# Down as seven whole products, its right parts made in gate/up, and layer 1's later modulation moved

## The chip, the cores and the metric

The kernel runs on one core of a Trainium2 chip. The metric is the device time of one execution in microseconds (us). Three executions of the kernel before took 2651.18 us in the median (2650.96 to 2657.16). One more execution was recorded by the profiler; it took 2657.73 us, of which the profile shows a span of 2656.0 us, at a granted TensorE clock of 0.974. All views of the trace come from that one. Engines: PE is TensorE's matmul, PEld its weight load, DVE VectorE, ACT ScalarE, POOL GpSimd, SP SyncE (here it issues nearly all DMAs, in the order in which they stand in its queue).

## The reference

Two layers of an encoder, one sequence of 1024 rows, width 1024, FFN width 2816, all in fp32:

```python
cond = silu(c)
for l in range(2):
    mod = cond @ w_mod[l] + b_mod[l]
    sh_a, sc_a, gt_a, sh_f, sc_f, gt_f = split(mod, 6)      # six groups of 1024
    h = rms_norm(x, g_attn[l]) * (1 + sc_a) + sh_a
    qa, ka, va, qb, kb, vb, qc, kc, vc = split(h @ w_in[l])
    ya = neighborhood_attention(qa, ka, va, rpb_na[l])       # group A
    yb = sliding_window_attention(qb, kb, vb, sink_sw[l], t5_table)   # group B
    yc = axial_attention(qc, kc, vc, gq_ax[l], gk_ax[l])     # group C
    y = concat(rms_norm(ya), rms_norm(yb), rms_norm(yc))
    x = x + gt_a * (y @ w_o[l])
    h = rms_norm(x, g_ffn[l]) * (1 + sc_f) + sh_f
    gate, up = split(h @ w_gu[l], 2)
    x = x + gt_f * ((silu(gate) * up) @ w_down[l])           # "down"
return rms_norm(x, g_final)
```

The six groups of `mod` are numbered (layer, 0) to (layer, 5) below: (1,0) and (1,1) are the shift and scale of layer 1's attention norm, (1,2) is the gate of its output projection, (1,3) to (1,5) belong to its FFN.

## The kernel before

**Numbers.** TensorE multiplies fp32 data in a faster form of lower precision (`F32R`), so each operand is split into a high part (a copy in `F32R`, made by ACT) and a low part (the source minus the high part, made by DVE or POOL): `split_to`, line 195. One product of tiles is three matmuls, high·high, low·high and high·low (`mm3`, line 187). The activations are kept transposed: rows of a tile are features (128 of them, a "block"), columns are the 1024 sequence positions in two halves of 512.

**Strassen–Winograd.** Gate/up and most of down don't compute the four quadrant products (feature blocks in pairs, sequence in halves) as eight multiplications but as seven, with sums of quadrants on both sides: `PRODUCTS`, line 203, gives for each of the seven its number, the name of its right part (`11`, `21`, `22`, `t1` to `t4`; the t are sums and differences of the quadrants b11, b12, b21, b22 of the right operand) and the PSUM bank into which it is added (a, b or c). `a_parts`, line 211, makes the seven left parts from raw weight tiles. `Ahead`, line 239, keeps up to eight such parts made ahead of the product that uses them; they live in the eight buffers of the tag `whl` (tiles `wpt`). Raw weights pass through the two buffers of `wst` (tiles `wr`, `wst`).

**Order.** Each engine runs its instructions in order. The order is what a scheduler makes of the program, except between `pin(..., True)` and `pin(..., False)`, where the order of the code is kept on the named engines. PSUM has eight banks, shared under the tag `mm` by all of `ps_w`, `ps_d`, `ps_mod`, `ps_ab` and so on.

**A layer's stages, in order.** Normed input h; projections of C (`ps_c`) and V (`ps_v`), then A and B (`ps_ab`, `ab_proj`/`ab_split`, whose results `qko` go to DRAM by `store()`); attention; output projection; gate/up; down; and the norm for the next stage.

**Modulation.** A group of `mod` takes eight steps (`mod_step`, line 283): a load of 128x1024 of `w_mod` (tile `wmt`, 512 KB; or two of 128x512) and a DVE operation that multiplies it by a scalar column of cond and adds it to `acc`. Then `acc` is split (`mod_parts`), summed over partitions on PE by a matmul with ones (`ps_mod`), picked on DVE by multiplying with the identity and reducing, and the bias is added (`mod_flush`, `mod_finish`). `mod_next` does a step each time it is called, the load and its use together. It is called in layer 0's V and A/B projections, its output projection and its gate/up, and there the six groups of layer 1 are made too.

**Gate/up.** 22 column groups q (even: gate, odd: up), each of 7 products of 12 matmuls. A pair of q gives 256 features of `silu(gate)*up`: the quadrants b11, b12 in a tile `e`, b21, b22 in a tile `o` (both `sg` in the trace), which `g_store` writes to DRAM (`gd`, 512 KB each).

**Down before.** 18 of the 22 feature blocks go through the seven products: for each of three stretches `kb` of 6 blocks, `g_load` reads them back (three loads of 1 MB, `graw`), `g_part` makes the seven right parts (sums and splits, on DVE and POOL in turn), and for `np2` in 0, 1 the weights of four output blocks are loaded in pieces of 384 KB and summed (`a_parts`, `dn_sums`). After every product its bank is added to the residual stream at once (`residual`, DVE `xb<-ps_w,mod,xb`, times the gate of the FFN): 84 of these a layer. The last 4 blocks are multiplied plainly (`down`, `down_block`; `ps_d`, 192 matmuls and 32 residuals). Half 0 of the next norm, or of the final norm, is started beside the last of these.

The part of the gate/up loop and of down that sets what runs when:

```python
for i, p in enumerate(PRODUCTS[2 if q < EARLY else 0 :]):
    gu_product(q, p, ahead.get())
    ahead.fill()
    if q + 1 < NF:
        g_store()
    elif i == 0:
        pin([sp], True)
    if i % 2 == 0 and l == 0 and q > 1:
        mod_next(psl, (ntp, "sq", 2, H))
```

## Time and profile before

| what | value |
|---|---|
| median of three runs | 2651.18 us |
| profiled execution / its span | 2657.73 / 2656.0 us |
| gate/up of layer 0 / layer 1, from its first product part to the last matmul | 471 us (631.80 to 1103.07) / 452 us (1925.00 to 2377.39) |
| down of layer 0 / layer 1 | 262 us (1103.07 to 1364.83) / 265 us (2377.39 to 2642.10) |
| C and V projections of layer 1 | 132 us (1364.83 to 1496.70) |
| A/B projections of layer 0 / layer 1 | 72 us (191.9 to 264.3) / 68 us (1496.70 to 1564.60) |
| after layer 1's down | 14 us |

How to read the rows that follow: a row of the engine totals gives busy time, share of the span and the number of instructions. In the groups, `out<-in` names the tiles without buffer numbers, `L47` is the line of the recording helper through which every operation passes (so all have the same line, and groups are told apart by their tiles), and behind the bars stand busy time and mean ns of one, then the engine's idle time ahead of them and what ended most of it. The chain of waits is followed back from the last instruction. The windows view gives start and end in us from the span's start. Sizes of the transfers that matter here:

```profile
gd<-sg SPq DMA_DIRECT2D x44, 512.0 KB, 3.1
graw<-gd SPq DMA_DIRECT2D x18, 1024.0 KB, 5.7
wmt<-in_w_mod_dram SPq DMA_DIRECT2D x98, 256.0 KB, 2.9
```

### The profile page before, as it was taken

Reading aid. Unit: us, or ns where it says so; the run is one execution under the profiler, and the core shown is the slowest. Engines: PE = TensorE matmul, PEld = TensorE weight load, DVE = VectorE, ACT = ScalarE, POOL = GpSimd, SP = SyncE. Lnnn points to the kernel's source line nnn. Section 1 sums busy time; section 2 is a strip of 40 time slices with the busy share of each in tenths; the row PEclk is TensorE's granted clock in tenths of the full one; section 3 lists DMA queues with packets and bytes.
Section 4 is the critical chain, followed back from the end, with each engine's and each line's share of the span. In section 5 each row is a group of like instructions: output and inputs, shape, how many; then the busy total and the mean of one; then the engine's idle time right before and its main releaser. Section 6 shows DMA issues by size and latency. Waiting matters only on the chain.

```text
span 2656.0 us, 34702 instructions
## 1 busy us (share of the span) xinstructions
PE 2481.2 (93%) x12055; PEld 2028.6 (76%) x12055; DVE 1918.7 (72%) x2964; ACT 1236.8 (47%) x2345; POOL 1193.6 (45%) x1039
## 2 busy tenths in 40 slices
PE   6899999898899999989999999999989999998898
PEld 4677898777688787667777879987867888876677
DVE  6845999987877777598778149998684443449876
ACT  5421888833433333343233148886444333334332
POOL 5641445543644444464345224455454444446431
PEclk9999999999999999999999999999989999998999
DMA  8467215074344554522233531241623222252222
GB/s 260 147 187 223 67 25 154 21 236 149 105 149 151 164 166 135 188 98 92 92 104 86 128 115 25 62 122 60 215 63 111 79 96 64 91 185 89 95 80 79
DMA packets 233566, 316.10 MB, mean 119 GB/s; under 512 B 29752, under 2 KB 166160, under 8 KB 233392
## 3 DMA queue, kind: packets, MB, share of 16 engines
q1 hardware_dynamic: 233088, 313.75, 37.9%
q8 instruction: 95, 1.56, 0.2%
q14 instruction: 79, 0.65, 0.1%
q0 software_dynamic: 304, 0.14, 0.0%
HBM read 244.24 MB, written 70.55 MB: 119 GB/s over the span
## 4 chain that ended last, share of the span: by engine, by line
PE 63%; DVE 23%; issue 4%; DMA 4%; ACT 3%; POOL 2%; SPq 0%; POOLq 0%; DVEq 0%; ACTq 0%
PE ps_w L47 29%; PE pv L47 6%; PE ps_ab L47 5%; PE ps_o L47 5%; PE T L47 4%; DVE xb L47 4%; PE ps_v L47 3%; PE sC L47 3%; PE ps_d L47 3%; DVE ws L47 2%; DVE wpt L47 2%; DMA wmt<-in_w_mod_dram 2%; DVE graw L47 2%; DVE acc L47 1%; PE sA L47 1%
## 5 line engine op out<-in xcount | busy, mean ns | idle before, releaser
L47 POOL TENSOR_SCALAR pr<-pr,rs 128x1024 f32<-128x1024 f32 (+4 forms) x256 | 208.8, 818 | 223.6 <-DVE rs L47 207.8
L47 POOL TENSOR_TENSOR wlo<-wst,whi 128x1024 fp32r<-128x1024 f32 x66 | 164.6, 2497 | 299.9 <-ACT whi L47 261.8
L47 POOL TENSOR_TENSOR wpt<-ws,wpt 128x512 fp32r<-128x512 f32 (+1 forms) x136 | 179.9, 1326 | 259.6 <-ACT wpt L47 215.4
L47 ACT CAST wpt<-ws 128x512 fp32r<-128x512 f32 (+1 forms) x272 | 155.8, 583 | 164.0 <-PE ps_w L47 77.5
L47 PE MATMUL pv<-pt,vs 128*128 128x256 f32 x1216 | 201.7, 297 | 11.3 <-DVE y L47 4.9
L47 POOL TENSOR_TENSOR wpt<-wr,wpt 128x512 fp32r<-128x512 f32 (+1 forms) x92 | 130.5, 1420 | 175.9 <-ACT wpt L47 150.5
L47 DVE TENSOR_TENSOR pt<-T,pt 128x512 fp32r<-128x512 f32 x304 | 199.4, 680 | 10.3 <-ACT pt L47 8.8
L47 PE MATMUL T<-identr,pr 128*128 128x128 f32 x1320 | 192.6, 275 | 4.9 <-POOL pr L47 1.9
L47 DVE TENSOR_TENSOR ws<-wr 128x512 f32<-128x512 f32 (+1 forms) x136 | 125.0, 925 | 92.0 <-POOL wpt L47 78.0
L47 ACT CAST pt<-T 128x512 fp32r<-128x512 f32 x304 | 170.1, 587 | 41.7 <-PE T L47 39.8
L47 POOL TENSOR_TENSOR sg<-sg,u 128x512 f32<-128x512 f32 x88 | 127.1, 1444 | 137.1 <-ACT u L47 68.1
L47 PEld LDWEIGHTS pv<-pt,vs 128*128 128x128 f32 x1216 | 161.5, 190 | 25.8 <-DVE y L47 12.7
L47 PEld LDWEIGHTS T<-identr,pr 128*128 128x128 f32 x1320 | 157.2, 141 | 27.1 <-POOL pr L47 4.4
L47 ACT COPY u<-ps_w 128x512 f32<-128x512 f32 x132 | 77.4, 586 | 215.7 <-PE ps_w L47 215.7
L47 DVE SCALAR_TENSOR_TENSOR acc<-wmt,condT,acc 128x512 f32<-128x512 f32 (+1 forms) x113 | 129.3, 1152 | 56.3 <-DMA wmt<-in_w_mod_dram 55.7
L47 DVE TENSOR_TENSOR wpt<-ws,wpt 128x512 fp32r<-128x512 f32 (+1 forms) x136 | 116.9, 860 | 64.4 <-ACT wpt L47 64.3
L47 DVE SCALAR_TENSOR_TENSOR xb<-ps_w,mod,xb 128x512 f32<-128x512 f32 x168 | 123.5, 742 | 48.3 <-PE ps_w L47 48.2
L47 ACT CAST wpt<-wr 128x512 fp32r<-128x512 f32 (+1 forms) x184 | 105.3, 578 | 112.1 <-PE ps_w L47 97.8
L47 ACT CAST whi<-wst 128x1024 fp32r<-128x1024 f32 x82 | 85.6, 1049 | 129.3 <-PE ps_o L47 40.5
L47 PE MATMUL ps_w<-ht3h,wpt 128*128 128x512 f32 x352 | 113.8, 405 | 17.4 <-ACT sg L47 16.0
L47 DVE TENSOR_REDUCE rs<-sC 128x1 f32<-128x1024 f32 x96 | 116.9, 1220 | 10.1 <-PE sC L47 9.8
L47 PE MATMUL ps_w<-ht2h,wpt 128*128 128x512 f32 x352 | 114.2, 405 | 7.7 <-ACT wpt L47 3.1
(332 smaller groups left out, 7127.2 us busy)
## 6 DMA issues: line engine op xcount, KB each, us to landing
wr<-in_w_gu_dram SPq DMA_DIRECT2D x92, 512.0 KB, 3.6
wmt<-in_w_mod_dram SPq DMA_DIRECT2D x98, 256.0 KB, 2.9
qk<-qkd SPq DMA_DIRECT2D x44, 512.0 KB, 7.2
gd<-sg SPq DMA_DIRECT2D x44, 512.0 KB, 3.1
wr<-in_w_down_dram SPq DMA_DIRECT2D x48, 384.0 KB, 3.6
graw<-gd SPq DMA_DIRECT2D x18, 1024.0 KB, 5.7
qkd<-qko SPq DMA_DIRECT2D x64, 256.0 KB, 3.5
wst<-in_w_o_dram SPq DMA_DIRECT2D x32, 512.0 KB, 4.2
```

Of the source, the lines that this page charges most:

```text
L47: ins = op(*args, **kwargs)
```

## The change

Four things change. In numbers for the whole program: matmuls in down go from 948 to 924 a layer, DVE's instructions from 2966 to 2898, POOL's from 1044 to 886, and SP's DMAs from 800 to 992.

**Down's loops.** The seven products run one after the other, in a new order (`DOWN`: numbers 1, 2, 6, 7, 4, 5, 3), each over all 22 feature blocks (11 pairs t) and four output blocks j. A step is a "unit", 77 in all: one left part and one right part of 128x512 are split (ACT and DVE; POOL isn't used), and 12 matmuls go into four banks. Products 1, 6, 7 and 4 share four banks (`acc_a`), 2, 5 and 3 the other four. A product's banks are added to the residual stream when it ends: 28 residuals a layer instead of 116.

**Weights.** All quadrants of the weights are loaded once, as 256 KB tiles `W[name, t]` that stay in SBUF (44 tiles, and 11 of `22` read a second time by `w_again`); the four sums are made in place on DVE (`w_sums`, `w_sum4`), at units that the table `due` names.

**Right parts.** The sums and differences of b11 to b22 are made in gate/up (`g_steps`, four subtractions on DVE per pair of column groups), and seven parts of 256 KB are stored to `gpd` in place of two of 512 KB to `gd`. Down reads them two units at a time (`b_load`, 512 KB) into the two buffers of `wst`.

**Modulation.** In gate/up `mod_stream` takes the place of `mod_next`: it issues each load one step ahead of its use, and stops ahead of group (1,2). The groups (1,2) to (1,5) are made in layer 1 instead, in the loops of its V and A/B projections, with three calls of `mod_next` after each A/B projection (layer 0 has one call there, as before). The norm of half 0 (`early_half`) runs beside products 5 and 3, and so do the squares of odd blocks of half 1.

The core of the diff:

```diff
+    DOWN = (
+        (1, "11", "a"), (2, "21", "b"), (6, "t2", "a"), (7, "t3", "a"), (4, "t4", "a"),
+        (5, "t1", "c"), (3, "22", "c"),
+    )
+    PLACE = {p[1]: i * NB for i, p in enumerate(DOWN)}
...
+    def mod_stream(psp, shared, until):
+        pl, tag, bufs, width = shared
+        acc = None
+        while todo and todo[0] < until:
+            l, g = todo[0]
...
+            if halves:
+                load(0)
+                yield
+            for i, (k, c0) in enumerate(halves):
+                if i + 1 < len(halves):
+                    load(i + 1)
+                mod_add(k, acc[:, c0 : c0 + width], loads.pop(i))
+                yield
+            going["step"] = KC
+            mod_parts(slice(0, width), shared)
+            yield
+            while going["step"]:
+                mod_flush(psp)
+                yield
...
-            if l == 0 and t > 1:
-                mod_next(psl, (ab, "zt", 4, 1024))
+            if t > 1:
+                mod_next(psl, (ab, "zt", 4, 1024), l)
...
-                for _ in range(1 - l):
-                    mod_next(psl, (ab, "zt", 4, 1024))
+                for _ in range(1 + 2 * l):
+                    mod_next(psl, (ab, "zt", 4, 1024), l)
...
+        def g_steps(b, e, o):
+            b11, b12, b21, b22 = (t[:, i * H : (i + 1) * H] for t in (e, o) for i in range(2))
+            def put(name, src):
+                sp.dma_start(gpd[:, PLACE[name] + b, :], src)
+            due = {
+                0: lambda: [put(*a) for a in (("11", b11), ("22", b22), ("21", b21))],
+                6: lambda: sub(b11, b12, b11),
+                7: lambda: (sub(b12, b22, b12), sub(b22, b22, b11), put("t1", b11)),
+                8: lambda: (sub(b21, b21, b22), put("t3", b12), put("t2", b22)),
+                9: lambda: put("t4", b21),
+            }
...
             for i, p in enumerate(PRODUCTS[2 if q < EARLY else 0 :]):
                 gu_product(q, p, ahead.get())
                 ahead.fill()
-                if q + 1 < NF:
-                    g_store()
-                elif i == 0:
-                    pin([sp], True)
-                if i % 2 == 0 and l == 0 and q > 1:
-                    mod_next(psl, (ntp, "sq", 2, H))
+                g_step()
+                if i % 2 == 0 and q > 1:
+                    next(mods_due, None)
...
+        def b_load(i):
+            n = min(2, NU - 2 * i)
+            t = wp.tile([P, 2, H], F32, name="graw", tag="wst", bufs=2)
+            sp.dma_start(t[:, :n], gpd[:, 2 * i : 2 * i + n, :])
+            for k in range(n):
+                raw[2 * i + k] = t[:, k]
+        A_SRC = ("11", "12", "11", "21", "11", "22", "12")
+        def units():
+            for u in range(NU):
+                i, t = divmod(u, NB)
+                both = []
+                for src in (W[A_SRC[i], t], raw.pop(u)):
+                    d = wp.tile([P, 2, H], F32R, name="wpt", tag="whl", bufs=8)
+                    split_to((d[:, 0], d[:, 1]), src, dve)
+                    both.append(d)
+                yield both
+        def w_sums(t):
+            w11, w21, w22 = (W[name, t] for name in ("11", "21", "22"))
+            dve.tensor_tensor(out=w22, in0=w21, in1=w22, op=ALU.add)
+            sub(w21, w11, w21)
+            sub(w11, w22, w11)
...
+        for t in range(NB):
+            at_unit(t, lambda t=t: w_first("12", t, wbp))
+            at_unit(4 + 2 * t, lambda t=t: w_first("21", t, wap))
+            at_unit(4 + 2 * t, lambda t=t: w_first("22", t, wbp))
+            at_unit(8 + 2 * t, lambda t=t: w_sums(t))
+            at_unit(31 + t, lambda t=t: w_sum4(t))
+            at_unit(33 + t, lambda t=t: w_again(t))
...
+        pin([sp], True)
+        for t in range(NB):
+            w_first("11", t, wap)
+            if t in (1, 3):
+                b_load(t // 2)
+        ahead = Ahead(units())
+        ahead.fill(4)
+        g_step(len(steps))
+        xt = blocks(xp)
+        b_load(2)
...
+        for u in range(NU):
+            i, t = divmod(u, NB)
+            num, _, bank = DOWN[i]
+            for what in due.get(u, ()):
+                what()
+            ahead.fill(4)
+            if u % 2 == 0 and (u + 6) // 2 <= (NU - 1) // 2:
+                b_load((u + 6) // 2)
...
+            banks = acc_a if bank == "a" else acc_b
+            a, b = ahead.have.pop(0)
+            for j in range(4):
+                js = slice(j * P, (j + 1) * P)
+                mm3(
+                    banks[j], a[:, 0, js], a[:, 1, js], b[:, 0], b[:, 1],
+                    num in (1, 2, 5) and t == 0, t == NB - 1, skip_group_check=True,
+                )
+            next(beside, None)
...
+            for j in range(4):
+                residual(banks[j], 2 * j + m, slice(half * H, half * H + H), 40)
+            if num == 4:
...
+                beside = chain(early_half(), odd_squares())
```

**Where down starts, on SP.** The first place at which the order differs is the end of layer 1's gate/up and the start of its down, in SP's queue of DMAs. Before (`wr` are raw weights, `graw` loads of the FFN's activations, `xb` blocks of the residual stream):

```order
L47 DMA wr<-in_w_gu_dram 128x4x256
L47 DMA xb<-xd 128x1024
L47 DMA graw<-gd 128x2x1024 x3
L47 DMA wr<-in_w_down_dram 128x3x256 x2
L47 DMA gd<-sg 128x1024 x2
L47 DMA xb<-xd 128x1024 x4
```

After the change (with buffer numbers; `sg_20511` is the last `e`, `sg_20512` the last `o`, `w11` the left weights of product 1):

```order
L49 DMA gpd_94<-sg_20511 128x512
L49 DMA gpd_94<-sg_20512 128x512
L49 DMA w11_20767<-in_w_down_dram 128x4x128
L49 DMA w11_20769<-in_w_down_dram 128x4x128
L49 DMA gpd_94<-sg_20512 128x512
L49 DMA graw_20771<-gpd_94 128x1024
L49 DMA w11_20773<-in_w_down_dram 128x4x128
L49 DMA w11_20775<-in_w_down_dram 128x4x128
L49 DMA graw_20777<-gpd_94 128x1024
```

The loads of the first activations stood ahead of the last two stores and read earlier blocks; now the third store of the last pair (part `21`) stands ahead of the first load of right parts.

**The same place, on DVE.** After the change, DVE's rows around that store (`u` are the results of an up product, `ps_w` its bank; the multiplication that finishes part `21` is the row `sg_20512<-sg_20512,ps_w_20645`):

```order
L49 TENSOR_TENSOR u_20691<-u_20691,ps_w_20693 128x512
L49 TENSOR_TENSOR sg_20511<-sg_20511 128x512
L49 TENSOR_TENSOR sg_20511<-sg_20512,sg_20511 128x512
L49 TENSOR_TENSOR sg_20512<-sg_20512,sg_20511 128x512
L49 TENSOR_TENSOR sg_20512<-sg_20512,ps_w_20645 128x512
L49 TENSOR_TENSOR wpt_20793<-w11_20767,wpt_20793 128x512
L49 TENSOR_TENSOR sg_20512<-sg_20512 128x512
L49 TENSOR_TENSOR wpt_20796<-graw_20771,wpt_20796 128x512
```

Three subtractions that overwrite b11, b12 and b22 stand ahead of the multiplication of the last product; the first split of a weight part stands between it and the fourth subtraction.

**Layer 1's A/B stage, on DVE.** The second place is behind the last split of V in layer 1 (`vs`). Before:

```order
L47 CAST qk<-pk 128x128
L47 TENSOR_TENSOR vs<-ps_v,vs 128x8x64 x8
L47 SCALAR_TENSOR_TENSOR qko<-ps_ab,qko 128x512 x12
L47 TENSOR_REDUCE rs<-sC 128x1 x2
L47 RECIPROCAL rs<-rs 128x1 x2
```

After the change the steps of a modulation group (`acc<-wmt,condT`) and its end stand between the results of the A/B projections (`qko`), and three more groups like it follow:

```order
L49 TENSOR_TENSOR vs<-ps_v,vs 128x8x64 x8
L49 TENSOR_SCALAR acc<-wmt,condT 128x1024
L49 SCALAR_TENSOR_TENSOR acc<-wmt,condT,acc 128x1024 x2
L49 SCALAR_TENSOR_TENSOR qko<-ps_ab,qko 128x512
L49 SCALAR_TENSOR_TENSOR acc<-wmt,condT,acc 128x1024 x5
L49 CAST acch<-acc 128x1024
L49 TENSOR_TENSOR accl<-acc,acch 128x1024
L49 TENSOR_TENSOR acc<-ps_mod,identr 128x512 x2
L49 TENSOR_REDUCE sums<-acc 128x4 x2
L49 TENSOR_TENSOR mod_83<-sums,vecs_81 128x8
```

On PE each of these groups puts four `ps_mod` matmuls between the A/B matmuls; the first stands behind 24 of them, the further ones 72, 72 and 48 apart.

342 lines of the change are left out of this document (147 added, 195 removed).

## The prediction

> **What bounds the kernel now.** I read the page first: its engine totals and its chain of waits.
>
> ```profile
> span 2656.0 us, 34702 instructions
> PE 2481.2 (93%) x12055; PEld 2028.6 (76%) x12055; DVE 1918.7 (72%) x2964; ACT 1236.8 (47%) x2345; POOL 1193.6 (45%) x1039
> PE 63%; DVE 23%; issue 4%; DMA 4%; ACT 3%; POOL 2%; SPq 0%; POOLq 0%; DVEq 0%; ACTq 0%
> ```
>
> PE carries 63% of the chain and DVE 23%, so the question for each stage is where the 23% sits. The windows view, cut at the first and last matmul of each stage, answers that: start and end, length, then the busy time of PE, PEld, DVE, ACT and POOL, the granted clock, DMA share and GB/s.
>
> ```profile
> 631.80:761.30 129.50, 108.21 (x437) 85.34 (x436) 107.66 (x120) 54.49 (x92) 67.59 (x42) 0.92 0.35 112
> 761.30:1085.80 324.50, 321.73 (x1379) 258.74 (x1378) 243.55 (x304) 119.05 (x211) 142.67 (x97) 1.00 0.48 154
> 1925.00:2045.50 120.50, 106.85 (x433) 84.74 (x432) 87.06 (x97) 52.35 (x90) 64.06 (x41) 0.93 0.27 89
> 2045.50:2360.20 314.70, 314.70 (x1356) 255.10 (x1356) 130.06 (x157) 120.21 (x211) 130.43 (x97) 1.00 0.26 85
> 1103.07:1364.83 261.76, 234.08 (x962) 182.11 (x960) 221.74 (x294) 96.23 (x177) 119.10 (x84) 0.96 0.31 103
> 2377.39:2642.10 264.71, 240.99 (x991) 187.91 (x990) 225.16 (x297) 94.30 (x176) 112.97 (x81) 0.95 0.27 93
> 1364.83:1496.70 131.87, 126.32 (x577) 101.61 (x576) 83.72 (x113) 45.39 (x87) 65.74 (x56) 0.96 0.38 102
> 1496.70:1564.60 67.90, 67.90 (x293) 54.65 (x292) 8.94 (x14) 12.05 (x18) 10.54 (x5) 1.00 0.49 131
> ```
>
> Rows 1 and 2 are gate/up of layer 0, rows 3 and 4 the same of layer 1, rows 5 and 6 down of the two layers, row 7 the C and V projections of layer 1, row 8 its A/B projections. Gate/up of layer 1 is a pure PE stage from 2045 on. Down is not: PE idles 28 and 24 us there and DVE is busy 85% of it. The A/B row has PE at 100% and DVE almost free.
>
> **The change part by part.**
>
> *Down, PE.* From the chain of waits, in order of time, two long unbroken stretches give the price of a matmul (start, length, count):
>
> ```profile
> 2009.18 362.80 PE ps_w L47 x1560
> 2594.11 34.00 PE ps_d L47 x150
> ```
>
> 362.8/1560 is 0.2326 us; 34.0/150 is 0.2267. Before, a layer's down has 756 matmuls in products and 192 plain ones, 948; after, 77 units of 12, 924. At 0.2326 a unit is 2.79 us and 77 of them 214.9 us (209.5 at the lower price). So the matmuls saved are worth only 6 us; the rest of the 262 and 265 us is waiting, and what matters is whether DVE keeps up.
>
> *Down, DVE.* It gains 2 splits a unit (154), 44 weight sums and 28 residuals: 226 instructions a layer; it loses 116 residuals, the sums and differences of the right parts, and its share (half each, POOL has the rest) of the splits of right and weight parts. POOL loses all its work in down. The tile view gives min/median/max of such a 128x512 operation in ns:
>
> ```profile
> L47 DVE TENSOR_TENSOR graw<-graw x36: 674/683/1787, 1111.9 to 2523.5; 128x512 f32<-128x512 f32 x36
> L47 DVE TENSOR_TENSOR ws<-wr 128x512 f32<-128x512 f32 (+1 forms) x136 | 125.0, 925 | 92.0 <-POOL wpt L47 78.0 <-DMA wr<-in_w_gu_dram 9.3 <-DMA wr<-in_w_down_dram 1.8
> L47 DVE SCALAR_TENSOR_TENSOR xb<-ps_w,mod,xb 128x512 f32<-128x512 f32 x168 | 123.5, 742 | 48.3 <-PE ps_w L47 48.2
> ```
>
> The median is 0.683, the mean of another group 0.925, and the largest 1.79. Residuals, one of whose sources is PSUM, never vary (0.742). I take 0.69, because POOL will be idle: 198 x 0.69 + 28 x 0.742 is 157 us of 215. The busy part is products 1 to 3: there DVE has 72 splits, 44 sums and 12 residuals, 128 operations, 89 us against 33 units or 92 us, with four units made ahead as a cushion. So it fits, barely. At 0.925 it would not: 118 us, a rival below.
>
> The Trainium skill, SBUF — State Buffer, "Who interferes with whom", says that a DVE operation with two SBUF inputs and a GpSimd operation that reads SBUF lock each other out for a whole instruction. By it the spread is POOL's doing and down would run at the low price, as summed; without it 0.925 would be as good a choice, and the sum 36 us longer. The spread in the trace fits it; no row here shows a down without POOL.
>
> *The start of down is a new wait.* On SP the third store of the last up block's tiles stands ahead of the first load of the right parts. It waits for the last product of gate/up, whose DVE multiplication now stands behind three subtractions; one of them waits until the store of block 22 has landed. From the timeline and the DMA table:
>
> ```profile
> 1102.84 0.39 PE L47 MATMUL ps_w<-ht4l,wpt 128*128 128x512 f32 x1
> 1101.33 1.54 POOL L47 TENSOR_TENSOR sg<-sg,u 128x512 f32<-128x512 f32 x1 [0.28 <-DVE u L47]
> t<-gd SPq DMA_DIRECT2D x16, 256.0 KB, 3.0
> wr<-in_w_gu_dram SPq DMA_DIRECT2D x92, 512.0 KB, 3.6
> L47 ACT CAST wpt<-ws x272: 506/620/630, 674.4 to 2573.3; 128x512 fp32r<-128x512 f32 x88, 128x384 fp32r<-128x384 f32 x48
> ```
>
> The last matmul ends at 1103.2; the store of 22 can go at about 1101.1 and lands 3.0 later; two operations of 0.69 bring DVE to 1105.5; issue of the store and of the load take until 1106.3; 3.6 to land, 0.62 for ACT's cast: unit 0 starts at about 1110.6, 7.4 us late, and units 2 and up follow from the next load. What PE does after such a gap is in the trace too:
>
> ```profile
> 1977.23 1.22 PE L47 MATMUL ps_w<-ht3h,wpt 128*128 128x512 f32 x2 [6.55 <-ACT sg L47]
> 1977.23 4.90 PE ps_w L47 x12
> ```
>
> After 6.55 us of idling 12 matmuls took 4.90 us, 2.1 more than 12 x 0.2326. Start: 7.4 + 2.1, near 10 us in each layer (bounds 0, if the load overtakes, and 14).
>
> *Other waits in down.* Product 7 adds into the banks that product 6 has just filled, 4 after 7 and 3 after 5: each first matmul waits for a residual. Four residuals take 3.0 us, the other three banks' matmuls 2.1: 1 us each, 3. Transfers: in the first 28 units about 24 MB (44 weight blocks, 18 loads of two units, 8 of x), 24/88 us or 270 GB/s. The trace moved more:
>
> ```profile
> 1097.00:1101.00 4.00, 4.00 (x19) 3.22 (x18) 0.43 (x1) 1.73 (x3) 2.54 (x2) 1.00 1.02 417
> ```
>
> so I take it as hidden but for 2 us a layer (bounds 0 and 10). The norm beside products 5 and 3 costs PE 8 small matmuls in layer 0, about 2 us with its wait, and 32 transposes in layer 1, 4 us.
>
> Layer 0: 215 + 10 + 3 + 2 + 2 = 232, against 261.8: **-30**. Layer 1: 215 + 10 + 3 + 2 + 4 = 234, against 264.7: **-31**. The tail behind it keeps its chain of residual, square, sum, scale and store: 0.
>
> ```profile
> 2642.10:2656.00 13.90, 4.73 (x41) 4.20 (x39) 5.67 (x10) 2.93 (x6) 3.71 (x3) 0.79 0.41 151
> ```
>
> *Between the layers.* Half 0 is now normed inside down; before, PE waited for its last chunks and for the second sum:
>
> ```profile
> 1374.45 1.62 DVE ssq L47
> 1379.55 4.37 PE ps_c L47 x12
> ```
>
> 12 matmuls in 4.37 us show PE slow after that wait, which is behind the chunks of half 0 and eight sums on DVE. In the change four squares are made by ACT and summed by PE, behind 24 matmuls that cover them: **-5** (bounds 0 and -9).
>
> *Gate/up.* Layer 0 sheds four of its six modulation groups. Its steady part was 324.5 against 314.7 in layer 1; two groups remain, with each load issued a step ahead of its use: **-8**. The early part differs by 9 more, but that comes from steps ahead of it, which stay:
>
> ```profile
> 629.52 2.69 DVE acc L47
> ```
>  Both layers gain 4 subtractions per 14 products (2.7 us in 39); DVE is 41% busy in layer 1, so PE hides them; +1 for the early rows, where it is not.
>
> *The moved modulation.* Layer 1's A/B stage now gets 32 loads of 512 KB and four groups of DVE work. Layer 0's A/B stage has the same work thinner (min/median/max of that stage alone, then one group's end; the rows at 1496.74 and on `ps_ab` say what layer 1 has):
>
> ```profile
> L47 DVE SCALAR_TENSOR_TENSOR acc<-wmt,condT,acc x15: 1274/1276/3306, 194.1 to 263.6; 128x1024 f32<-128x1024 f32 x15
> DMA to landing us min/median/max: 3.9/5.4/7.5
> 252.87 0.69 DVE L47 CAST acch<-acc 128x1024 fp32r<-128x1024 f32 x1
> 253.67 1.22 DVE L47 TENSOR_TENSOR accl<-acc,acch 128x1024 fp32r<-128x1024 f32 x1
> 256.54 1.29 DVE L47 TENSOR_TENSOR acc<-ps_mod,identr 128x512 f32<-128x512 f32 x2 [1.64 <-PE ps_mod L47]
> 257.75 1.27 DVE L47 TENSOR_REDUCE sums<-acc 128x4 f32<-128x512 f32 x2
> 177.38 19.65 SPq L47 DMA_DIRECT2D wmt<-in_w_mod_dram  x7
> 1496.74 0.69 DVE L47 TENSOR_TENSOR vs<-ps_v,vs 128x512 fp32r<-128x512 f32 x1 [4.91 <-ACT vs L47]
> L47 PE MATMUL ps_ab<-hl,whi x256: 387/393/628, 93.8 to 1562.9; 128*128 128x512 f32 x128
> ```
>
> PE's order puts each group's four ps_mod matmuls behind 24, 72, 72 and 48 A/B matmuls, and PE goes in order: it waits there for the group's last step. DVE starts when the last V block is split, 0.7 us into row 8 (1497.4). Its chain to the fourth ps_mod: 28 steps at 1.28 and 4 first ones at 0.75 (38.8), four ends of 0.69 + 1.22 + 1.29 + 1.27 with 1.2 of waiting for PE (22.7, less 4 of the last one, which come behind its matmuls), 9 low halves of projections at 0.69 (6.2), and some 7 us where POOL's weight splits stretch a step to 3.3 as above: 71 us, to 1568. Then 72 matmuls (16.7) and 2 us of slow PE: 1587, where row 8's PE ends at 1562.9. **+25.** Loads keep up: four buffers, 5.4 to land and 1.3 to use, one every 1.7 us against the chain's 2.2. Bounds: +4, the 16 ps_mod matmuls alone, if DVE hid the rest; +45 at one load every 3 us.
>
> Sum: -30 - 31 - 5 - 8 + 1 + 25 = **-48 us** on the span of 2656.0, so 2608. The profiled execution took 2657.7 (span and 1.7 around it), 6.5 more than the median of the runs, 2651.2; on that median, **2603 us**.
>
> **The rivals.**
>
> *DVE binds down.* If sums and splits cost 0.925 though POOL is idle, products 1 to 3 take 118 us instead of 92, less a cushion of 8: 18 us a layer, 2639. For it: DVE has 3% to spare there. Against: medians of 0.68 beside a busy POOL. 0.14.
>
> *The moved modulation is hidden.* DVE had 59 of 68 us free in that stage; if PE's waits shrink to the 16 matmuls, 2582. Against: the first ps_mod comes after one projection block, 5.6 us, and needs eight steps. 0.08.
>
> *The start of down is not late.* If the loads overtake the stores, 20 us less: 2583. Against: SP's order. 0.08.
>
> *Slower.* The modulation loads of the A/B stage go one at a time: on SP each three stand between stores of qko halves that wait for DVE, so buffers that are free are filled late. One at a time a load costs 5.4 + 0.4 + 1.3, 7.1 us; 28 of them are 199, and the stage ends 130 us later than I have it: 2733. It decides from about 4.4 us a load, where the time passes 2659. For it: SP is in order. Against: layer 0 issued seven in 20 us on the same queue. 0.06.
>
> **How the numbers follow.** My own case (2590 to 2625) has 0.64, the rivals 0.14, 0.08, 0.08 and 0.06. The range of 2578 to 2642 takes in the two faster rivals, the lower matmul price and the DVE rival. A measurement here tells 0.3%, 8 us. Faster by more: all but the slower rival and part of DVE's case, 0.88; within: 0.06; slower: 0.06.
>
> **What would show it.** In down of the changed kernel: units 2.79 us apart, PE idle about 7 us ahead of the first, the wait ending in ACT's cast or the load of graw; DVE's 128x512 operations at 0.69 with POOL empty; residuals 28 a layer. In layer 1's A/B stage: PE idle ahead of each ps_mod on DVE, the first about 10 us, the stage near 92 us long. Wrong it would be if down is longer than 245 us, or if the A/B stage stays under 75.

## The result and the profile after

The changed kernel took 2649.16 us in the median of 20 runs (2637.84 to 2656.60) and the kernel before 2652.38 us in the same series: a ratio of 0.9985, interval 0.9974 to 0.9997. That is 3 us faster, just clear of the noise, where 48 were forecast. The profiled execution took 2648.72 us. The page of the changed kernel, with the span, the engine totals (busy time, share, instructions) and the shares of the chain of waits, answers to the first lines of the prediction:

```profile
span 2646.6 us, 34697 instructions
...
PE 2467.0 (93%) x12071; PEld 2037.8 (77%) x12071; DVE 1809.6 (68%) x2896; ACT 1241.2 (47%) x2335; POOL 964.5 (36%) x881
...
PE 50%; DVE 6%; issue 4%; DMA 2%; ACT 2%; POOL 1%; SPq 1%; POOLq 0%; DVEq 0%; ACTq 0%
```

The totals say that DVE and POOL have less to do and that PE is busy just as large a part of the time. They don't say why the time stayed. (The chain isn't comparable as a whole: its shares add up to 66% here, and near the end it runs through stretches in which POOL had nothing to do.) The windows view of the changed kernel, cut at each stage's last matmul, does. Rows: full products of layer 0's gate/up, layer 0's down, layer 1's C and V projections, its A/B projections, the full products of its gate/up, its down, the tail.

```profile
761.50:1110.60 349.10, 337.96 (x1437) 272.15 (x1435) 190.36 (x242) 120.79 (x214) 138.96 (x100) 0.99 0.35 113
1110.60:1334.80 224.20, 213.96 (x938) 175.81 (x938) 162.23 (x253) 102.87 (x178) 12.88 (x10) 0.98 0.66 198
1334.80:1479.40 144.60, 134.96 (x606) 109.93 (x605) 71.62 (x101) 42.91 (x83) 61.50 (x52) 0.92 0.40 112
1479.40:1584.00 104.60, 81.95 (x306) 62.94 (x305) 72.45 (x73) 11.02 (x16) 13.43 (x5) 0.85 0.70 226
2070.70:2402.60 331.90, 331.90 (x1429) 268.89 (x1427) 152.72 (x192) 121.08 (x214) 134.37 (x100) 1.00 0.29 96
2402.60:2628.00 225.40, 217.63 (x968) 179.22 (x967) 157.10 (x246) 98.98 (x173) 4.27 (x3) 0.98 0.64 190
2628.00:2646.60 18.60, 9.92 (x73) 9.34 (x71) 4.38 (x8) 3.54 (x7) 3.71 (x3) 0.66 0.30 113
```

Layer 0's gate/up before, cut in the same way (the prediction's row ends sooner, at 1085.80):

```profile
761.30:1103.00 341.70, 338.93 (x1453) 272.60 (x1452) 245.39 (x307) 123.16 (x218) 148.23 (x102) 1.00 0.50 160
```

Set against the profile before, from each stage's last matmul to the next one's:

| stage | before | after | difference | forecast |
|---|---|---|---|---|
| up to the end of layer 0's output projection | 631.9 | 630.9 | -1.0 | 0 |
| gate/up 0, first products / full products | 129.4 / 341.7 | 130.6 / 349.1 | +8.6 | -8 |
| down 0 | 262.0 | 224.3 | -37.7 | -30 |
| C and V of layer 1 | 131.1 | 144.5 | +13.4 | -5 |
| A/B of layer 1 | 67.2 | 104.6 | +37.4 | +25 |
| attention and output projection 1 | 361.9 | 362.5 | +0.6 | 0 |
| gate/up 1, first products / full products | 120.3 / 331.8 | 124.2 / 331.9 | +4.0 | +1 |
| down 1 | 264.8 | 225.4 | -39.4 | -31 |
| tail | 13.9 | 18.6 | +4.7 | 0 |
| sum | 2656.0 | 2646.6 | -9.4 | -48 |

The gain in down came, and was larger than forecast: 77 us. Five other rows gave 68 us of it back, 37 of them the A/B stage. (On the medians the change is worth 3 us instead of the 9.4 of these two executions; executions of one kernel differ by that much.)

**The A/B stage** is where most of it went. The timeline of PE in the changed kernel (start, length, operation; in brackets idle time before it and what ended it) at the ps_mod matmuls of the first three groups:

```profile
1494.01 1.22 PE L49 MATMUL ps_mod<-acch,onesr 128*128 128x512 f32 x2 [8.99 <-DVE acch L49]
...
1519.15 1.19 PE L49 MATMUL ps_mod<-acch,onesr 128*128 128x512 f32 x2 [5.44 <-DVE acch L49]
...
1542.21 1.22 PE L49 MATMUL ps_mod<-acch,onesr 128*128 128x512 f32 x2 [2.42 <-DVE acch L49]
```

PE waits for DVE's groups, as forecast, 22.5 us in all. But DVE waits too. The groups of DVE in that stage, with idle time ahead of them in the last column:

```profile
L49 DVE SCALAR_TENSOR_TENSOR qko<-ps_ab,qko 128x512 fp32r<-128x512 f32 x11 | 7.6, 690 | 22.6 <-ACT qko L49 22.6
...
L49 DVE TENSOR_TENSOR acc<-ps_mod,identr 128x512 f32<-128x512 f32 x8 | 5.2, 686 | 2.9 <-PE ps_mod L49 2.9
```

DVE stood idle 22.6 us ahead of the low halves of projections, some 12 of them before its fourth group was done. All but 1.5 of these 12 fall behind the first ps_mod: there DVE waited for projections that PE was late with, since PE had waited for DVE's group before it began them.

**The C stage** has a new wait. The chain of waits in it (start, length, what):

```profile
1366.49 1.30 POOL hl L49
1367.81 0.37 SPq L49
...
1368.82 12.00 DMA cst<-const_rope_dram
```

The last chunk of the norm ends on POOL at 1367.8, and only then SP issues the loads of the q/k gains and rotary constants, which take 12.00 us to land. That is 33 us behind the end of down (1334.8). Before the change the same loads went out 9 to 15 us behind it (1364.8), ahead of the norm's chunks of half 1:

```profile
1376.14 3.38 SPq L47 DMA_DIRECT2D cst<-const_rope_dram  x5
```

**Layer 0's gate/up** has stalls that layer 1's, with the same products and stores, doesn't have. The longest, in the timelines of DVE, ACT and PE:

```profile
916.18 2.49 DVE L49 TENSOR_TENSOR sg<-sg 128x512 f32<-128x512 f32 x2 [1.18 <-POOL sg L49]
918.59 0.68 DVE L49 TENSOR_TENSOR sg<-sg,ps_w 128x512 f32<-128x512 f32 x1
919.19 0.68 DVE L49 TENSOR_TENSOR wpt<-wr,wpt 128x512 fp32r<-128x512 f32 x1
919.79 0.69 DVE L49 TENSOR_TENSOR sg<-sg 128x512 f32<-128x512 f32 x1
921.62 0.69 DVE L49 TENSOR_TENSOR sg<-sg 128x512 f32<-128x512 f32 x1 [1.14 <-DMA gpd<-sg]
922.22 0.68 DVE L49 TENSOR_TENSOR u<-u,ps_w 128x512 f32<-128x512 f32 x1
...
922.94 0.63 ACT L49 ACTIVATE sg<-u 128x512 f32<-128x512 f32 x1 [9.29 <-DVE u L49]
...
924.10 1.22 PE L49 MATMUL ps_w<-ht3h,wpt 128*128 128x512 f32 x2 [5.58 <-ACT sg L49]
```

Read from below: PE waits 5.58 us for ACT, ACT 9.29 us for DVE's addition of `u`, and ahead of that addition DVE has the four new subtractions (`sg<-sg`), two of which wait themselves, for POOL's multiplication and for a store that still reads what they overwrite.

### The profile page after: what moved, and what is told of

It reads as the page before. It is cut to its first block, busy times and chain, and to the rows that moved or that the text cites. A ratio compares the mean times of both kernels' runs of the same rounds, so it can differ in the third digit from the quotient of the medians.

```text
span 2646.6 us, 34697 instructions
## 1 busy us (share of the span) xinstructions
PE 2467.0 (93%) x12071; PEld 2037.8 (77%) x12071; DVE 1809.6 (68%) x2896; ACT 1241.2 (47%) x2335; POOL 964.5 (36%) x881
## 4 chain that ended last, share of the span: by engine, by line
PE 50%; DVE 6%; issue 4%; DMA 2%; ACT 2%; POOL 1%; SPq 1%; POOLq 0%; DVEq 0%; ACTq 0%
PE ps_w L49 21%; PE ps_d L49 13%; PE ps_o L49 3%; PE pv L49 3%; PE ps_ab L49 2%; PE T L49 2%; PE ps_v L49 2%; PE sC L49 1%; DVE xb L49 1%; DVE acc L49 1%; PE ps_st L49 1%; SPq L49 1%; ACT pr L49 0%; DMA cst<-const_rope_dram 0%; PE sA L49 0%
## 5 line engine op out<-in xcount | busy, mean ns | idle before, releaser
L49 PE MATMUL ps_d<-wpt 128*128 128x512 f32 x1848 | 428.2, 393 | 18.0 <-ACT wpt L49 17.7
L49 PEld LDWEIGHTS ps_d<-wpt 128*128 128x128 f32 x1848 | 348.4, 189 | 93.4 <-ACT wpt L49 18.3
L49 DVE TENSOR_TENSOR pt<-T,pt 128x512 fp32r<-128x512 f32 x304 | 199.7, 681 | 10.2 <-ACT pt L49 8.6
L49 POOL TENSOR_TENSOR wpt<-ws,wpt 128x512 fp32r<-128x512 f32 x88 | 119.5, 1360 | 217.9 <-ACT wpt L49 133.4
L49 ACT CAST wpt<-w 128x512 fp32r<-128x512 f32 x154 | 95.5, 620 | 171.6 <-PE ps_d L49 155.5
L49 DVE TENSOR_TENSOR wpt<-w,wpt 128x512 fp32r<-128x512 f32 x154 | 108.3, 703 | 77.7 <-ACT wpt L49 77.4
L49 DVE TENSOR_TENSOR wpt<-ws,wpt 128x512 fp32r<-128x512 f32 x88 | 78.5, 892 | 102.6 <-ACT wpt L49 102.5
L49 DVE TENSOR_TENSOR ws<-wr 128x512 f32<-128x512 f32 x88 | 86.3, 981 | 90.5 <-POOL wpt L49 81.0
L49 ACT CAST wpt<-ws 128x512 fp32r<-128x512 f32 x176 | 108.2, 622 | 78.7 <-PE ps_w L49 37.6
L49 DVE SCALAR_TENSOR_TENSOR acc<-wmt,condT,acc 128x1024 f32<-128x1024 f32 (+1 forms) x85 | 116.6, 1375 | 27.0 <-DMA wmt<-in_w_mod_dram 26.1
L49 DVE TENSOR_TENSOR wpt<-graw,wpt 128x512 fp32r<-128x512 f32 x154 | 108.9, 707 | 28.6 <-ACT wpt L49 28.6
```

Of the source, the lines that this page charges most:

```text
L49: ins = op(*args, **kwargs)
```

## The experiments

Twelve kernels. Stage lengths are from the one profiled execution of each, medians and ratios to the kernel before from the timed runs. In stages that a kernel's edit doesn't touch, the full products of layer 0's gate/up spread from 345.8 to 351.7 us, C and V from 142.7 to 146.2, A/B from 104.6 to 105.2: differences below that are no evidence.

| kernel | median, us | ratio [interval] | gate/up 0, full | down 0 | C, V | A/B | down 1 |
|---|---|---|---|---|---|---|---|
| before | 2652.4 | 1 | 341.7 | 262.0 | 131.1 | 67.2 | 264.8 |
| changed | 2649.2 | 0.9985 [0.9974, 0.9997] | 349.1 | 224.3 | 144.5 | 104.6 | 225.4 |
| before_mod_moved | 2685.9 | 1.0129 [1.0110, 1.0149] | 335.2 | 262.6 | 131.0 | 108.0 | 263.6 |
| mod_back | 2630.5 | 0.9921 [0.9907, 0.9935] | 371.9 | 224.5 | 144.6 | 66.9 | 226.2 |
| mod_flush_late | 2622.6 | 0.9899 [0.9881, 0.9917] | 348.4 | 223.6 | 142.3 | 83.5 | 225.8 |
| mod_back_pool_subs | 2621.0 | 0.9887 [0.9869, 0.9905] | 360.9 | 223.6 | 143.6 | 66.9 | 225.1 |
| after_pool_subs | 2639.0 | 0.9949 [0.9928, 0.9969] | 341.2 | 223.3 | 142.7 | 105.0 | 225.4 |
| stores_no_wait | 2638.0, one run | - | 345.6 | 224.1 | 144.1 | 104.9 | 225.8 |
| rope_early | 2642.1 | 0.9963 [0.9951, 0.9975] | 351.7 | 224.2 | 135.0 | 105.0 | 225.4 |
| loads_first | 2649.8 | 0.9990 [0.9979, 1.0001] | 347.4 | 225.2 | 144.5 | 105.2 | 227.1 |
| loads_first_2 | 2649.7 | 0.9988 [0.9974, 1.0003] | 347.5 | 223.0 | 146.2 | 105.0 | 225.4 |
| loads_first_2_fewer | 2633.7, one run | - | 350.8 | 214.7 | 145.0 | 104.9 | 215.8 |
| pool_busy_in_down | 2726.4 | 1.0283 [1.0262, 1.0303] | 345.8 | 262.1 | 143.9 | 105.2 | 265.2 |
| best | 2607.4 | 0.9819 [0.9796, 0.9842] | 340.1 | 223.2 | 136.8 | 82.7 | 226.1 |

### The modulation move alone, and undone

before_mod_moved, on the kernel before:

```diff
-    def mod_next(psp, shared):
+    def mod_next(psp, shared, until=(2, 0)):
...
-        if not todo or going["step"] == KC:
+        if not todo or todo[0] >= until or going["step"] == KC:
...
-            if l == 0 and t > 1:
+            if t > 1:
                 mod_next(psl, (ab, "zt", 4, 1024))
...
-                for _ in range(1 - l):
+                for _ in range(1 + 2 * l):
                     mod_next(psl, (ab, "zt", 4, 1024))
...
-                    mod_next(psl, (ntp, "sq", 2, H))
+                    mod_next(psl, (ntp, "sq", 2, H), (1, 2))
```

> The kernel before with only the modulation groups (1,2) to (1,5) moved into layer 1's V and A/B loops (three calls after each A/B projection), the rest as before. Theory: the move alone costs some 37 us in layer 1's A/B stage and gives back 4 us in layer 0's gate/up: 2652 + 33 = 2685 us, ratio 1.012. Rival: the A/B stage of the changed kernel is long for another reason that came with the rest of the change (later transfers, other buffers); then this kernel is within 5 us of the kernel before, ratio 0.998 to 1.002.

It came out as the theory had it: 2685.9 us, 33.5 more than before. The windows of that kernel, gate/up 0 and the A/B stage of layer 1:

```profile
761.50:1096.70 335.20, 335.17 (x1437) 269.57 (x1436) 165.49 (x207) 123.97 (x218) 138.40 (x102) 1.00 0.34 113
1490.30:1598.30 108.00, 81.32 (x304) 62.22 (x302) 72.51 (x73) 11.12 (x16) 12.57 (x5) 0.86 0.68 219
```

Four groups less give gate/up back 6.5 us, PE then being busy all of it; the A/B stage pays 41 us. The A/B stage's price is the move's alone.

mod_back, on the changed kernel, undoes it:

```diff
-            if t > 1:
+            if l == 0 and t > 1:
                 mod_next(psl, (ab, "zt", 4, 1024), l)
...
-                for _ in range(1 + 2 * l):
+                for _ in range(1 - l):
...
-        mods_due = mod_stream(psl, (ntp, "sq", 2, H), (1, 2))
...
-                if i % 2 == 0 and q > 1:
-                    next(mods_due, None)
-        for _ in mods_due:
-            pass
+                if i % 2 == 0 and l == 0 and q > 1:
+                    mod_next(psl, (ntp, "sq", 2, H), 1)
```

> The changed kernel with layer 1's modulation made as before the change: all six groups in layer 0 (the steps in gate/up load and use at once, as before), none in layer 1's V and A/B loops. Everything else stays. Theory: the moved modulation alone is what ate most of the gain, because in layer 0's gate/up it cost PE only its ps_mod matmuls. Then layer 1's A/B stage falls from 104.6 to about 68 us (-37), gate/up of layer 0 gains 16 ps_mod matmuls, 4 us, and the time is about 2649 - 33 = 2616 us, ratio to before 0.987. Rival: with the four subtractions per pair of column groups DVE can no longer carry six groups in gate/up; then the A/B stage falls the same, but gate/up of layer 0 (349 us from its first full product to its last matmul) grows by 15 to 30 us, ratio 0.992 to 0.998.

The rival was right about the size: the A/B stage is back at 66.9 us, but gate/up of layer 0 takes 371.9, 30 more than the kernel before with the same modulation in it. What fills DVE's queue there isn't the modulation alone; it is the modulation together with what the change put into gate/up.

### Who holds up gate/up

mod_back_pool_subs and after_pool_subs put the four subtractions on POOL, the one on mod_back, the other on the changed kernel:

```diff
-                6: lambda: sub(b11, b12, b11),
-                7: lambda: (sub(b12, b22, b12), sub(b22, b22, b11), put("t1", b11)),
-                8: lambda: (sub(b21, b21, b22), put("t3", b12), put("t2", b22)),
+                6: lambda: sub(b11, b12, b11, pool),
+                7: lambda: (sub(b12, b22, b12, pool), sub(b22, b22, b11, pool), put("t1", b11)),
+                8: lambda: (sub(b21, b21, b22, pool), put("t3", b12), put("t2", b22)),
```

> The kernel mod_back (layer 1's modulation all in layer 0, as before the change) with one more edit: the four subtractions per pair of column groups run on POOL instead of DVE. mod_back's stretch of full products in layer 0's gate/up took 371.9 us, against 341.7 before and 349.1 in the changed kernel, and PE waited there for ACT's and DVE's clearing of its banks. Theory: the subtractions do the harm because they stand in DVE's queue, ahead of the operations that clear PE's banks, and wait there for POOL's multiplications and for stores to land; on POOL they are off that path, the stretch falls to 345 to 352 us, and the time is about 2608 us, ratio 0.984. Rival: it is SP's queue, in which 154 stores that wait for results stand ahead of the loads of weights and of w_mod; then the stretch stays within 6 us of 372 and the ratio at 0.992.

> The changed kernel with only the four subtractions per pair of column groups on POOL instead of DVE. In the changed kernel the stretch of full products of layer 0's gate/up took 349.1 us; the kernel before with only the modulation moved, which has the same two groups there but no parts to make, took 335.2. Theory: DVE's queue with the waiting subtractions is half of this or more, as it was in mod_back: the stretch falls to 338 to 342 us, ratio 0.9955. Rival: with two groups DVE has room, and the 14 us are SP's: the stretch stays at 347 us or more, ratio 0.9985.

With six groups the stretch went from 371.9 to 360.9 us, half of what the theory asked for; with two, from 349.1 to 341.2, within the theory's range. The windows of after_pool_subs:

```profile
761.00:1102.20 341.20, 335.61 (x1437) 269.26 (x1435) 173.08 (x214) 121.01 (x214) 181.95 (x133) 1.00 0.36 116
```

PE is idle 5.6 us there instead of 11.1, although POOL has 43 us more to do. With the subtractions on it DVE was busy for only 190 of the 349 us, so it was less their work that did the harm than their place in DVE's queue, where they wait. But 6 us stay over the 335.2 of before_mod_moved with two groups, and 19 over the 341.7 of before with six; these are not explained.

stores_no_wait asked whether that is SP's queue:

```diff
+                if b < NB - 1:
+                    src = f32(hb["11"][0][:, 0])
                 sp.dma_start(gpd[:, PLACE[name] + b, :], src)
```

> The changed kernel in which the stores of right parts in gate/up (all but those of the last pair) take their data from a tile that has long been ready, so that they move the same bytes in the same places of SP's queue but wait for nothing, and the subtractions wait for no store; the subtractions stay on DVE. It leaves the real right parts out of down for ten of the eleven pairs. If SP's queue (weights and w_mod loads behind stores that wait) makes the 14 us of layer 0's gate/up, its stretch falls from 349 to 335 to 338 us. If DVE's subtractions make them, it stays at 345 us or more.

345.6 us is the second outcome, at the lower end of the spread of kernels that don't touch this stage, and PE still waits 7.4 us for ACT there (11.1 in the changed kernel). So SP's waiting stores aren't the main cause; whether they are the rest, one run doesn't tell.

### The A/B stage: two queues that wait in turn

mod_flush_late leaves all work in the stage, puts the parts of `acc` into the buffers `whl`, and lets a group's ps_mod matmuls stand about one group later in PE's order (`mod_late` is called in place of `mod_next` in layer 1):

```diff
+    def mod_late(psp, shared):
+        if pend:
+            pend[0][0] += 1
+            if pend[0][0] > 5:
+                _, (l, g), hi, lo = pend.pop(0)
...
+        if going["step"] == KC:
+            _, hi, lo, _ = going["parts"]
+            pend.append([0, todo.pop(0), hi, lo])
+            going["step"] = 0
+        if todo:
+            going["at"] = wp, "whl", 8
+            mod_next(None, shared, 1)
```

> The changed kernel with the ps_mod matmuls of each group in layer 1's A/B stage issued about one group later (six calls), so that PE reaches them when DVE has long finished the group; same work otherwise, the parts of acc lie in the weight-part buffers. In the changed kernel that stage took 104.6 us: PE waited 22.5 us ahead of ps_mod for DVE, and DVE stood idle some 13 us for projection results of PE. Theory: the two in-order queues wait for each other in turn; with the matmuls late neither waits and the stage takes PE's own 76 us and some 8 for the last group, 84 us: 2629 us, ratio 0.991. Rival: DVE's own chain (32 steps and four ends) or the w_mod loads are the bound; the stage stays above 97 us: 2642 us or more, ratio 0.996 to 0.9985.

The stage fell to 83.5 us and the time to 2622.6. The window of the stage in this kernel:

```profile
1482.40:1565.90 83.50, 75.80 (x305) 59.53 (x303) 69.59 (x73) 11.37 (x16) 11.14 (x5) 0.94 0.82 268
```

and DVE's group of low halves in it, with the idle time ahead of them:

```profile
L49 DVE SCALAR_TENSOR_TENSOR qko<-ps_ab,qko 128x512 fp32r<-128x512 f32 x11 | 7.6, 687 | 3.6 <-ACT qko L49 3.6
```

PE's group of ps_mod matmuls, first in the changed kernel, then here:

```profile
L49 PE MATMUL ps_mod<-acch,onesr 128*128 128x512 f32 x8 | 4.8, 704 | 22.5 <-DVE acch L49 22.5
L49 PE MATMUL ps_mod<-acch,onesr 128*128 128x512 f32 x8 | 3.2, 460 | 7.2 <-DVE acch L49 7.2
```

DVE has the same 70 us of work, the transfers are the same 32 loads, and both waits are mostly gone: DVE's for projections went from 22.6 to 3.6 us, PE's for DVE from 22.5 to 7.2. That the parts of `acc` lie elsewhere leaves the loads more buffers, but it isn't what helped: DVE's idle time ahead of the steps that use the loads rose, from 1.0 to 3.4 us. So of the 37 us that the stage had grown by, 21 were neither DVE's work nor the loads, but the alternation. The other 16 stay: PE is busy for 75.8 us where it was 67.9 before the change, and idle for 7.7.

### The rotary constants

rope_early swaps two pools on their stack:

```diff
-        nt_cm, ntp = open_pool("nt", side="left")
         wa_cm, wap = open_pool("wa", side="right")
         wb_cm, wbp = open_pool("wb", side="left")
+        nt_cm, ntp = open_pool("nt", side="left")
```

> The changed kernel with the pools of the norm's tiles and of the weights 12 and 22 in the other order on their stack, so that the rotary constants and q/k gains of layer 1 no longer take the place of tiles that the norm still uses. Theory: in the changed kernel these loads are issued at 1367.8 us, after the norm's last chunk, and land 12 us later; issued early they are hidden, and the C stage of layer 1 is 9 to 11 us shorter: 2639 us, ratio 0.995. Rival: the first rotary product waits for something else as well (projections of C, the gains, DVE), and less than 3 us come off: ratio 0.998.

C and V took 135.0 us, 9.5 less, and the median is 7.1 lower. The loads now leave SP 14 us earlier, beside the norm (timeline of SP in this kernel):

```profile
1353.63 0.58 SPq L49 DMA_DIRECT2D g<-in_gq_ax_dram  x1
...
1354.84 2.91 SPq L49 DMA_DIRECT2D cst<-const_rope_dram  x5
```

So 9.5 us, of the 13.4 that this stage lost, were a matter of addresses: the loads' tiles lay where the norm's tiles had been, and waited for their last reader.

### The start of down

loads_first puts the last pair's stores behind the first two loads of right parts, loads_first_2 behind five (stores and subtractions then come at unit 2):

```diff
-                g_step()
+                if (q, i) != (NF - 1, 6):
+                    g_step()
...
-        g_step(len(steps))
-        xt = blocks(xp)
...
+            if u == 2:
+                g_step(len(steps))
+                xt = blocks(xp)
```

(The first three lines are loads_first; loads_first_2 has the rest too, and one load of the residual stream a unit later.)

> The changed kernel with the stores of the last pair's parts 11, 22 and 21 and its four subtractions put behind down's first loads, instead of ahead of them; nothing else. Theory: PE's wait of 7.6 us at the start of each down is the SP queue (the third store waits for the last multiplication, and the first load of right parts stands behind it), so both waits shrink to 1 or 2 us and PE isn't slowed after them: 8 us a layer, 2633 us, ratio 0.992. Rival: the first units then wait for weights or for the buffers that gate/up's raw weights still hold, and a wait of some 5 us stays: ratio 0.996 to 0.998.

> The changed kernel with all of the last pair's stores and subtractions put behind down's first five loads of right parts (loads_first had put them behind two, and PE's wait of 7.9 us at the start went down to 1.9, but a wait of 5.9 to 6.8 us came up behind the first 48 matmuls, ahead of the third load). Theory: the wait is SP's queue alone, and with the stores behind loads that aren't needed yet both waits go: down takes 217 us instead of 224.3 and 225.4, the time is about 2635 us, ratio 0.993. Rival: the transfers of the first products (DMA busy near 1.0 there) are the bound, so that what is won at the start is lost in the next units: down stays at 223 us or more, ratio 0.9985.

Both did to the first wait what was expected, and neither made down shorter. PE in layer 0's down, first in the changed kernel:

```profile
1118.45 12.77 PE L49 MATMUL ps_d<-wpt 128*128 128x512 f32 x48 [7.63 <-ACT wpt L49]
1132.96 164.16 PE L49 MATMUL ps_d<-wpt 128*128 128x512 f32 x720 [1.75 <-ACT wpt L49]
```

then in loads_first:

```profile
1114.55 12.80 PE L49 MATMUL ps_d<-wpt 128*128 128x512 f32 x48 [1.86 <-ACT wpt L49]
1133.24 166.71 PE L49 MATMUL ps_d<-wpt 128*128 128x512 f32 x720 [5.89 <-ACT wpt L49]
```

and in loads_first_2:

```profile
1116.81 27.98 PE L49 MATMUL ps_d<-wpt 128*128 128x512 f32 x120 [2.17 <-ACT wpt L49]
1150.04 149.66 PE L49 MATMUL ps_d<-wpt 128*128 128x512 f32 x648 [5.25 <-ACT wpt L49]
```

The wait wanders from unit 0 to unit 4 to unit 10 and keeps its 7 to 9 us in all. loads_first_2_fewer takes 5 MB a layer out of the loads of these units:

```diff
         def w_first(name, t, pl):
+            if t and name in ("21", "22"):
+                W[name, t] = W[name, 0]
+                return
```

> The kernel loads_first_2 with 20 of the 44 weight loads of down's first products left out a layer: the weights 21 and 22 are loaded for the first pair only and its tiles stand for those of the other ten, so 5 MB of 24 MB in the first 28 units aren't moved, and products 3, 4 and 6 in the table of down use wrong weights. If transfers bound the first 30 units (the wait of PE moved from unit 0 to unit 4 to unit 10 while the total stayed), the waits go and down takes 216 to 218 us in both layers instead of 223.0 and 225.4. If SP's order alone makes the wait at unit 10 (the sixth load behind the seven stores), it stays: 222 us or more.

Now the waits are gone, in both layers (windows of the two downs):

```profile
1114.90:1329.60 214.70, 212.40 (x938) 174.47 (x937) 158.36 (x246) 99.16 (x171) 13.03 (x10) 1.00 0.54 168
2398.90:2614.60 215.70, 215.47 (x967) 177.21 (x966) 152.84 (x239) 94.80 (x166) 4.90 (x4) 1.00 0.51 159
```

Down's first 30 units are bound by their loads: either the late start or the loads cost these 8 to 10 us, and mending the one uncovers the other. Whether it is the bytes or SP's time to issue 20 loads more, this run doesn't part. In the changed kernel both are busy nearly all the time there: the DMA engines' share in the first 60 us of layer 0's down was 0.92 to 1.13 in windows of 12 us, and from 1115.8 to 1157.6 SP issued with only one pause of 4 us.

### Why DVE kept up in down

pool_busy_in_down gives POOL something to do there:

```diff
+        busy = ntp.tile([P, H // 2], F32, name="busy")
+        pool.memset(busy, 0.0)
...
+            for _ in range(3):
+                pool.tensor_tensor(out=busy, in0=busy, in1=busy, op=ALU.add)
             next(beside, None)
```

> The changed kernel with useless work on POOL in both downs: 231 additions of a 128x256 tile to itself a layer, which nothing waits for (three a unit, some 185 us); all else stays. In the changed kernel POOL did nothing there and DVE's 128x512 splits took 0.70 to 0.71 us in the mean. Theory: the spread of DVE's operations with two SBUF inputs comes from POOL; with POOL busy the splits' mean rises to 0.9 us or more, DVE no longer keeps up in products 1 to 3, and down is 15 us or more longer a layer: 2680 us, ratio 1.01. Rival: the spread comes from transfers; the splits stay at 0.70 to 0.75 us and the time within 0.3% of the changed kernel's.

DVE's splits of weights (tile view: min/median/max ns), first in the changed kernel:

```profile
L49 DVE TENSOR_TENSOR wpt<-w,wpt x154: 675/693/1399, 1113.0 to 2617.8; 128x512 fp32r<-128x512 f32 x154
```

then with POOL busy:

```profile
L49 DVE TENSOR_TENSOR wpt<-w,wpt x154: 673/1095/1403, 1108.5 to 2690.5; 128x512 fp32r<-128x512 f32 x154
```

and the residuals of layer 0's down there:

```profile
L49 DVE SCALAR_TENSOR_TENSOR xb<-ps_d,mod,xb x28: 734/736/751, 1152.4 to 1367.7; 128x512 f32<-128x512 f32 x28
```

Operations with two sources in SBUF went from 0.69 to 1.10 us, those with one source in PSUM stayed at 0.74, and down grew from 224.3 to 262.1 us, as long as it was before the change; POOL was busy for 215 of them. A POOL that is idle in down is a condition of the gain. That the splits slow down and the residuals don't is what the Trainium skill's page "SBUF — State Buffer", section "Who interferes with whom", has as its rule, that GpSimd and a DVE operation that needs the port which they share exclude each other; the trace agrees, with these numbers.

### The best version found

best takes the changed kernel and the edits of mod_flush_late, rope_early and after_pool_subs.

> The changed kernel with three of the edits tried together: ps_mod matmuls of layer 1's A/B stage issued later (mod_flush_late), norm and weight pools swapped so that the rotary constants load early (rope_early), and the four subtractions per pair on POOL. Theory: the three stalls lie in different stages, so the savings add: 26.6 us from the first and 7.1 us from the second as their runs gave them, and about 6 us for the third in a gate/up that holds two groups only: 2609 us, ratio 0.984. Rival: the savings overlap (what one wins is waited for in the next stage), 2620 us or more, ratio 0.988.

2607.4 us, 0.9819 of the time before: the three savings (26.6, 7.1 and 10.2 us by their medians) add up to within some 2 us. Its stages: full products of gate/up 0, down 0, C and V, A/B:

```profile
759.50:1099.60 340.10, 334.79 (x1437) 269.97 (x1435) 172.90 (x214) 121.03 (x214) 182.74 (x133) 1.00 0.36 116
1099.60:1322.80 223.20, 214.80 (x938) 176.62 (x938) 160.06 (x249) 102.86 (x178) 18.38 (x14) 0.98 0.66 199
1322.80:1459.60 136.80, 131.66 (x606) 108.15 (x605) 71.76 (x101) 43.07 (x83) 61.37 (x52) 0.94 0.43 119
1459.60:1542.30 82.70, 75.22 (x305) 58.75 (x303) 70.10 (x73) 11.38 (x16) 11.19 (x5) 0.96 0.82 271
```

## Why the prediction was wrong

The forecast was 2603 us, range 2578 to 2642; 2649 lies outside. The largest term, down, was right in its mechanism. All five smaller terms came out slower than forecast; the steps that failed are the chain to the fourth ps_mod in the A/B stage, the norm between the layers, the step by which PE hides the subtractions in gate/up, and the tail. That the direction is right is partly luck: with the 61 us forecast for down in place of the 77 measured, the other rows as they came would have made the kernel slower (by 7 us on the two profiled executions).

- **Down (-61 forecast, -77 measured): right in its mechanism.** The price of a matmul was 0.228 us (164.16/720), near the lower of the two prices, where the sum took the upper: 4 us a layer. Of the three turns of the banks in a layer one shows a wait, 0.71 us in layer 0, where the sum had 3. DVE's splits took 0.70 to 0.71 us in the mean, near the 0.69 of the sum and not the rival's 0.925, and the reason given, POOL's idleness, is shown by pool_busy_in_down. (The sum's 128 operations for products 1 to 3 count all 44 weight sums; 9 of them come later, from unit 33 on, so DVE had some 6 us more room than it says.)
- **The start of down: right in place and size, wrong as a price.** PE waited 7.63 and 7.61 us (7.4 forecast) and was slow after it (in the first 4.63 us of layer 1's down it did 11 matmuls, at a granted clock of 0.50), with the chain as described: the third store, the load of right parts, ACT's cast. The rival that won 20 us without this wait was wrong, and so was the step "so I take it as hidden but for 2 us a layer": with the wait gone the loads hold PE up for nearly as long. The 417 GB/s by which they were called hidden were those of 4 us in another stage; in windows of 12 us these units moved at most 340 in layer 0 and 343 in layer 1.
- **The moved modulation (+25 forecast, +37.4 measured): the mechanism was right, a term was missing.** The sum took DVE's chain to the fourth ps_mod as almost all DVE's own work, 71 us, with the projections' results ready whenever DVE came to their low halves. It took 82.6 (from 1480.7 to 1563.3), because DVE waited some 12 us for these results, most of them late because PE had waited for DVE. mod_flush_late takes the waiting in turn away, and 21 of the 37 us with it, with the same work on DVE.
- **Between the layers (-5 forecast, +13.4 measured): the step failed.** It asked which work leads to the norm of half 1, and found that shorter; it didn't ask what the pools' new places do to the loads behind it. rope_early shows 9.5 us of the difference of 18. Of the rest nothing was tried. The likely part is the summing of the squares, which the step took as covered by 24 matmuls: PE does it in 40 small matmuls behind those 24, most of them behind a wait for the last squares, where the kernel before has 8 in 1.05 us.

```profile
1342.97 7.29 PE L49 MATMUL ps_st<-onesr,sq 128*128 128x1 f32 x34 [1.94 <-ACT sq L49]
```

- **Gate/up of layer 0 (-8 forecast, +8.6 measured): the first half right, the second wrong.** Four groups less are worth 6.5 us (before_mod_moved). The step "DVE is 41% busy in layer 1, so PE hides them" carried an average of layer 1 over to layer 0, where two groups of modulation still run and the subtractions wait in DVE's queue for POOL and for stores: 14 us, 8 of which after_pool_subs recovered. The other 6 are open, and so are 3 of layer 1's gate/up (+1 forecast, +4.0 measured, all in its first products).
- **The tail (0 forecast, +4.7 measured).** The sum of half 1's squares is now made by PE in 40 small matmuls where it was 8, in a row behind the last residual, and took 4.85 us longer. Before, and after:

```profile
2645.22 0.95 PE L47 MATMUL ps_st<-onesr,ssq 128*128 128x1 f32 x8
```

```profile
2631.01 5.80 PE L49 MATMUL ps_st<-onesr,sq 128*128 128x1 f32 x40
```

"The tail behind it keeps its chain" overlooked it. It was not tried separately.

Of the rivals, none came true. The range was too narrow because its bounds were drawn around the terms of the sum; three of the misses (the loads' addresses, the alternation, the squares on PE) weren't costs of uncertain size but waits and work that the sum didn't have.

## What to carry to other kernels

The modulation was moved to where DVE was idle, and PE paid for it, which waits in line for the result. Two in-order queues that each hold the other's next input added their waits, and moving the consumer one group later was worth 21 us with the same work. When pools are re-ordered, list which loads now lie on tiles that are released late. And before mending a visible wait, ask what it covers: down's start could be mended twice without gaining anything, because its loads held PE up for nearly as long.

## What was unexpected of the hardware

POOL's useless additions on a private tile of 1 KB a partition, with no dependence on anything, made DVE's splits, which have two SBUF sources, 58% longer (0.693 to 1.095 us in the median) and cost the kernel 77 us. That the effect would show was forecast, with 15 us or more a layer; that it alone would undo all of down's gain was not. That both layers came within 1 us of the time before is chance, since the number of additions was chosen freely.
